# Seven block products for eight in the branch projections of a hybrid encoder trunk

## The chip, the cores and the metric

The kernel runs on one NeuronCore of a Trainium2 chip. The metric is the device time of one execution in microseconds; the times of several runs are given by their median. All arithmetic is in float32: a matrix product is done as three matmuls on rounded parts (below).

## The reference, cut to what matters

Two layers work on x (256 tokens, 2048 channels). In a layer the normalised input h is projected by w_in (2048 columns in, 14848 out) to the inputs of three token mixers and to the merge gates. Each mixer's output (256 x 1024) is multiplied by a SiLU gate, projected to 2048 channels, and the three are merged with sigmoid gates:

```
ya = einsum('bse,ed->bsd', ya * silu(rg), w_ret)     # retention, w_ret 1024 x 2048
yb = einsum('bse,ed->bsd', yb * silu(pg), w_pool)    # pooling
yc = einsum('bse,ed->bsd', yc * silu(ag), w_att)     # windowed attention
gates = sigmoid(mg).reshape(B, S, 3, D)              # mg = h @ w_in[:, 8704:]
merged = gates[:, :, 0] * ya + gates[:, :, 1] * yb + gates[:, :, 2] * yc
x = x + einsum('bsd,de->bse', merged, w_out)
```

## The kernel before, in words

**Numbers.** Every operand of a product is split into a rounded part (hi, type float32r) and the remainder (lo = value - hi); a product is a_hi w_hi + a_hi w_lo + a_lo w_hi, all added up in PSUM. For weights, ScalarE makes hi (line 208) and VectorE makes lo (line 219); activations are split by split (lines 302 to 308).

**Weight tiles.** All weights come as tiles of 128 x 1024 values (512 KB) in the order of use, which _plan writes out. SyncE loads them to four buffers (raw, line 197); there are four buffers of hi and three of lo. weights() hands out the next tile and keeps the engines ahead: when TensorE is about to use tile i, the remainder of tile i+2, the rounding of tile i+3 and the loads up to tile i+6 have been issued. A buffer is free for the next when the last reader of the one before is done, so a remainder can start when TensorE has left the tile three earlier, a rounding when it has left the tile four earlier, and a load when the remainder four earlier is made.

**Products.** gemm_n (line 310) makes 256 tokens x 512 columns: for each weight tile (two blocks of 128 rows, 512 columns) and each half t of the tokens it issues two blocks x three matmuls, 12 a tile. gemm_t makes the transposed form (channels on partitions) that some inputs want.

**Side work.** Everything else is written as generators that Side steps: each tick(), once a weight tile, lets every live task emit its next few instructions, and `yield n` makes a task wait n ticks. So small work is spread between the tiles, in the order in which it is written. Small results in PSUM (mix) use four banks in turn, and the large products two buffers of two banks (acc).

**Order of a layer.** Attention's inputs, its gate, retention's q and k, v and gate; then pooling's inputs and gates (gemm_t) with its group maps; then the merge, lines 837 to 853: for each branch (attention, retention, pooling) and each of four column blocks c of 512, the merge gate (gemm_n over eight tiles, then a sigmoid on ScalarE) and the branch projection (gemm_n over four tiles), which merge_task multiplies by the gate and adds to merged[c]. In the last branch turn_task transposes merged[c] in two halves and splits them (mt). Then the output projection (gemm_n over mt, eight tiles a column block) and the residual. The second pooling map (pool_out(1)) stands behind the first merge gate of attention.

Of the kernel before, what the change touches and what calls it, by code (L numbers as in the profile page):

```python
# [16 lines left out]
P = 128  # L17
# [15 lines left out]
N_SLOTS = 25  # L33
N_RAW, N_HI, N_LO = 4, 4, 3
N_WAKE = 9


def _plan():


    def n_tiles(name, l, c0, nk):
        return [(name, l, k2 * 256, c0, 2, 512) for k2 in range(nk // 2)]

    def t_tiles(l, c0):
        return [("w_in", l, k4 * 512, c0, 4, 256) for k4 in range(KD // 4)]

    plan = []
    for l in range(DEPTH):
        plan += n_tiles("w_in", l, OFF["akv"], KD)
        for j in range(2):  # L50
            plan += n_tiles("w_in", l, OFF["aq"] + j * 512, KD)
        for j in range(4):
            plan += t_tiles(l, OFF["ag"] + j * 256)
        for h in range(RH):
            plan += t_tiles(l, OFF["rq"] + h * RD) + t_tiles(l, OFF["rk"] + h * RD)
        for part in ("rv", "rg"):
            for j in range(2):
                plan += n_tiles("w_in", l, OFF[part] + j * 512, KD)
        for g in range(4):
            plan += t_tiles(l, OFF["pv"] + g * 256)  # L60
        for g in range(4):
            plan += t_tiles(l, OFF["pg"] + g * 256)
            if g == 2:
                plan.append(("pool_w", l, 0, 0, 4, 256))
        for b, name in ((2, "w_att"), (0, "w_ret"), (1, "w_pool")):
            for c in range(4):
                plan += n_tiles("w_in", l, OFF["mg"] + b * D + c * 512, KD)
                if b == 2 and c == 0:
                    plan.append(("pool_w", l, 512, 0, 4, 256))
                plan += n_tiles(name, l, c * 512, KW)  # L70
        for c in range(4):
            plan += n_tiles("w_out", l, c * 512, KD)
    return plan


class Side:
# [36 lines left out]
def kernel(  # L113
# [23 lines left out]
    ps_m = ctx.enter_context(tc.tile_pool(name="ps_m", bufs=4, space=PSUM))  # L137

    uid = [0]

# [19 lines left out]
    def acc(s):  # L160
        return ps_a.tile([P, 2, 512], F32, tag="acc", name=nm(s))

    def mix(s):
        return ps_m.tile([P, 512], F32, tag="mix", name=nm(s))

    side = Side()
    start, tick = side.start, side.tick
# [13 lines left out]
        return task.value  # L181


    plan = _plan()
    raws, his, los = [], [], []
    used = [0]

    def load_to(n):
        while len(raws) < min(n, len(plan)):
            i = len(raws)  # L190
            kk, w = plan[i][4:]
            raw = wp.tile([P, kk, w], F32, tag="raw", name=nm("raw"), bufs=N_RAW)
            if i == 0:
                for k in range(kk):
                    nc.sync.dma_start(out=raw[:, k], in_=weight_tiles[i][:, k * w:(k + 1) * w])
            else:
                nc.sync.dma_start(out=raw.rearrange("p k e -> p (k e)"), in_=weight_tiles[i])
            raws.append(raw)

    def hi_to(n):  # L200
        while len(his) < min(n, len(plan)):
            i = len(his)
            hi = wp.tile(list(raws[i].shape), F32R, tag="whi", name=nm("whi"), bufs=N_HI)
            if i == 0:
                for k in range(hi.shape[1]):
                    nc.vector.tensor_copy(hi[:, k], raws[i][:, k])
            else:
                nc.scalar.copy(hi, raws[i])  # L208
            his.append(hi)

    def lo_to(n):
        while len(los) < min(n, len(plan)):
# [55 lines left out]
    def ps_col(l, k):  # L268
        return cols[:, 32 + l * KW + k:32 + l * KW + k + 1]

    rope = cp.tile([P, 2, S], F32, name="rope")
# [9 lines left out]
    def rest_task():  # L281
        yield 3
        for c in range(4):
            load_x(c * 512, 512)
            yield 1
        nc.sync.dma_start(out=gains[:, 0], in_=attn_q_gain.partition_broadcast(P))
        nc.sync.dma_start(out=gains[:, 1], in_=attn_k_gain.partition_broadcast(P))
        yield 1
        nc.sync.dma_start(out=rope, in_=c_rope)
# [20 lines left out]
    def gemm_n(act, nk, early=False):  # L310

        pt = [mix("pn0"), mix("pn1")] if early else acc("pn")
        n2 = nk // 2
# [16 lines left out]
        for k2 in range(n2):  # L330
# [13 lines left out]
            if early and k2 >= n2 - 2:  # L344
                kept.append((k2, a2, hi, lo, 1))
            else:
                products(k2, a2, hi, lo, 1)
            if k2 + 1 < n2:
                tick()
        for args in kept:  # L350
# [82 lines left out]
    def scales_task(ss):  # L433
# [53 lines left out]
    for l in range(DEPTH):  # L487
# [251 lines left out]
            ut_ret += [start(retain_task(2 * j + i, rg_t)) for i in range(2)]  # L739


        def pooled_task(g, pt):
            s, _ = yield from summed(pt)
            yield 1
# [71 lines left out]
        def merge_task(b, c, pt, gs):  # L816
            yield 1
            if b == 0:
                m = slot([P, 2, 512], F32, "mrg")
                merged.append(m)  # L820
                for t in range(2):
                    nc.vector.tensor_tensor(m[:, t], pt[:, t], gs[t], ALU.mult)
                return
            m = merged[c]
            for t in range(2):
                nc.vector.tensor_tensor(gs[t], pt[:, t], gs[t], ALU.mult)
                nc.vector.tensor_tensor(m[:, t], m[:, t], gs[t], ALU.add)

        def turn_task(c, j, merge_t):
            yield from until(merge_t)  # L830
            m = merged[c]
            yield 1 + j
            pm = transposed([m[:, t, (2 * j + i) * P:(2 * j + i + 1) * P] for i in range(2) for t in range(2)], "pmt")
            yield 1
            return split_t(pm, "mt")

        merged = []
        mt_tiles = []
        for b, ut in enumerate((ut_att, ut_ret, ut_pool)):
            for c in range(4):  # L840
                pt = gemm_n(ht, KD)
                gs = []
                for t in range(2):
                    g = half([P, 512], "mg")
                    nc.scalar.activation(g, pt[:, t], AF.Sigmoid, scale=sc(t))  # L845
                    gs.append(g)
                tick()
                if b == 0 and c == 0:
                    ut_pool += pool_out(1)
                merge_t = start(merge_task(b, c, gemm_n(ut, KW), gs))  # L850
                tick()
                if b == 2:
                    mt_tiles += [start(turn_task(c, j, merge_t)) for j in range(2)]


        last = l + 1 == DEPTH
# [52 lines left out]
def _laid_out(inputs):  # L909

    import numpy as np

    a = {name: np.asarray(v) for name, v in inputs.items()}
    x = a["x"]
    plan = _plan()
    tiles = np.empty((len(plan), P, 1024), np.float32)
    for i, (name, l, r0, c0, kk, w) in enumerate(plan):
        mat = a[name][l]
        if name == "pool_w":
            mat = mat.reshape(W, 256)  # L920
        tiles[i] = mat[r0:r0 + kk * P, c0:c0 + w].reshape(kk, P, w).transpose(1, 0, 2).reshape(P, kk * w)
# [55 lines left out]
```

## Time and profile before

| | |
|---|---|
| median of 3 runs | 1813.17 us (1813.15 to 1813.53) |
| profiled execution, its own time | 1813.54 us |
| its span, first to last instruction | 1811.7 us |
| TensorE matmuls | 1803.6 us busy, 8866 instructions |
| VectorE | 1105.4 us busy |
| ScalarE | 856.5 us busy |
| GpSimd | 19.0 us busy |
| DMA | 339.53 MB, mean 187 GB/s |

Busy time is the time in which an engine has an instruction under way; TensorE's matmuls are pipelined, so one matmul's duration is longer than the distance to the next. "Idle before, releaser" in the lists is the time that an engine stood still in front of such instructions and what ended it. The trace names engines PE (TensorE), PEld (its weight loads), DVE (VectorE), ACT (ScalarE), POOL (GpSimd) and SP (SyncE).

### The profile page before, as it was taken

The numbers are of one execution on the slowest core, as the hardware profiler recorded it, in microseconds if no ns is written. First come the engines' busy times: TensorE is split into PE (matmuls) and PEld (weight loads), VectorE is DVE, ScalarE is ACT, GpSimd is POOL, SyncE is SP. The second block draws the span as 40 slices with busy tenths as digits, with TensorE's granted clock in tenths as the row PEclk, the third lists the DMA queues.
The fourth block names the chain that finished last, engine by engine and source line by source line (L and its number), as shares of the span: only waits on it lengthen the run. The fifth ranks groups of instructions, "written<-read, shape, count | busy, mean of one in ns | idle before, by whom it ended". The sixth has DMA issues, their size and how long they took to land.

```text
span 1811.7 us, 23247 instructions
## 1 busy us (share of the span) xinstructions
PE 1803.6 (100%) x8866; PEld 1522.3 (84%) x8866; DVE 1105.4 (61%) x1356; ACT 856.5 (47%) x1087; POOL 19.0 (1%) x22
## 2 busy tenths in 40 slices
PE   9999999999999999999999999999999999999999
PEld 7888888888888888888888888888888888888887
DVE  6778865676444555555567788657754454555554
ACT  6455654445444444444444555544444444444432
POOL 0000000000000000000000000000000000000000
PEclk9999999999999999999999999999999999999999
DMA  8554455455555555555555544454555556555564
GB/s 321 191 196 168 155 164 185 164 189 191 192 194 196 190 195 189 193 188 186 185 186 186 187 163 163 163 185 164 186 196 190 195 190 197 194 192 188 189 199 150
DMA packets 95951, 339.53 MB, mean 187 GB/s; under 512 B 11104, under 2 KB 11744, under 8 KB 95840
## 3 DMA queue, kind: packets, MB, share of 16 engines
q1 hardware_dynamic: 95120, 337.11, 55.8%
q8 instruction: 69, 1.13, 0.3%
q10 hardware_dynamic: 720, 0.94, 0.2%
q14 instruction: 42, 0.34, 0.1%
HBM read 335.91 MB, written 2.10 MB: 187 GB/s over the span
## 4 chain that ended last, share of the span: by engine, by line
PE 99%; DMA 1%; DVE 0%; ACT 0%; DVEq 0%; issue 0%; ACTq 0%; SPq 0%
PE pn L322 69%; PE pt L366 16%; PE pt L369 8%; DMA raw<-in_weight_tiles_dram 1%; PE ppt L394 0%; PE pmt L394 0%; PE pqt L394 0%; DMA cols<-in_columns_dram 0%; PE pro L401 0%; PE py L401 0%; PE pss L401 0%; PE py L400 0%; PE psc L400 0%; PE psc L399 0%; PE py L399 0%; PE pss L400 0%
## 5 line engine op out<-in xcount | busy, mean ns | idle before, releaser
L219 DVE TENSOR_TENSOR wlo<-raw,whi 128x1024 fp32r<-128x1024 f32 x627 | 767.4, 1224 | 626.3 <-PE pn L322 495.9
L208 ACT CAST whi<-raw 128x1024 fp32r<-128x1024 f32 x627 | 660.3, 1053 | 765.6 <-PE pn L322 569.5
L322 PE MATMUL pn<-whi,ht 128*128 128x512 f32 x2424 | 748.7, 391 | 0.1
L322 PEld LDWEIGHTS pn<-whi,ht 128*128 128x128 f32 x2424 | 454.8, 188 | 94.2 <-ACT ht L419 0.6
L322 PE MATMUL pn<-wlo,ht 128*128 128x512 f32 x1212 | 460.0, 389 | 0.4 <-DVE wlo L219 0.4
L366 PE MATMUL pt<-ht,whi 128*128 128x512 f32 x1280 | 450.4, 397 | 0.0
L369 PE MATMUL pt<-ht,wlo 128*128 128x256 f32 x1280 | 353.3, 281 | 0.0
L366 PEld LDWEIGHTS pt<-ht,whi 128*128 128x128 f32 x1280 | 238.9, 188 | 53.1
L322 PEld LDWEIGHTS pn<-wlo,ht 128*128 128x128 f32 x1212 | 227.7, 188 | 47.0 <-DVE wlo L219 0.7
L369 PEld LDWEIGHTS pt<-ht,wlo 128*128 128x128 f32 x1280 | 241.5, 189 | 2.9
L322 PE MATMUL pn<-whi,mt 128*128 128x512 f32 x512 | 158.1, 391 | 0.0
L322 PEld LDWEIGHTS pn<-whi,mt 128*128 128x128 f32 x512 | 96.1, 188 | 19.8
L322 PE MATMUL pn<-wlo,mt 128*128 128x512 f32 x256 | 97.1, 389 | 0.0
L322 PE MATMUL pn<-whi,uta 128*128 128x512 f32 x256 | 77.5, 389 | 0.0
L322 PE MATMUL pn<-whi,utp 128*128 128x512 f32 x256 | 77.5, 389 | 0.0
L322 PE MATMUL pn<-whi,utr 128*128 128x512 f32 x256 | 77.4, 389 | 0.0
L322 PEld LDWEIGHTS pn<-whi,utp 128*128 128x128 f32 x256 | 48.1, 188 | 10.0
L322 PEld LDWEIGHTS pn<-whi,utr 128*128 128x128 f32 x256 | 48.1, 188 | 9.9
L322 PEld LDWEIGHTS pn<-wlo,mt 128*128 128x128 f32 x256 | 48.1, 188 | 9.8
L322 PEld LDWEIGHTS pn<-whi,uta 128*128 128x128 f32 x256 | 47.9, 188 | 9.8
L845 ACT ACTIVATE mg<-pn,rstd 128x512 f32<-128x512 f32 x48 | 30.4, 686 | 39.7 <-PE pn L322 39.7
L384 ACT COPY tb<-pt 128x512 f32<-128x512 f32 x40 | 23.4, 585 | 54.1 <-PE pt L366 54.0
(161 smaller groups left out, 1099.1 us busy)
## 6 DMA issues: line engine op xcount, KB each, us to landing
raw<-in_weight_tiles_dram SPq DMA_DIRECT2D x627, 512.0 KB, 3.3
xa<-in_x_dram SPq DMA_DIRECT2D x4, 512.0 KB, 6.6
out_dram<-o SPq DMA_DIRECT2D x7, 256.0 KB, 4.7
xt<-in_x_t_dram SPq DMA_DIRECT2D x5, 256.0 KB, 6.7
lag<-in_c_lag_dram SPq DMA_DIRECT2D x2, 512.0 KB, 4.3
xt<-in_x_t_dram ACTq DMA_DIRECT2D x3, 256.0 KB, 6.1
raw<-in_weight_tiles_dram SPq DMA_DIRECT2D x2, 256.0 KB, 5.2
inv<-in_c_inv_dram SPq DMA_DIRECT2D x1, 512.0 KB, 4.2
```

What stands on the lines that cost most here:

```text
L208: nc.scalar.copy(hi, raws[i])
L219: nc.vector.tensor_sub(lo, raws[i], his[i].bitcast(F32))
L322: nc.tensor.matmul(pt[t] if early else pt[:, t, :], lhsT=a2[:, kk, ai, ts], rhs=w[:, kk], start=k2 == 0 and n == 0, stop=k2 == n2 - 1 and ...
L366: nc.tensor.matmul(pt[:, e, :], lhsT=hi[:, kk, es], rhs=a.rearrange("p h n -> p (h n)"), start=start, stop=stop)
L369: nc.tensor.matmul(pt[:, e, 0:S], lhsT=lo[:, kk, es], rhs=a[:, 0, :], start=False, stop=False)
L384: nc.scalar.copy(b, pt[:, :, S:2 * S])
L845: nc.scalar.activation(g, pt[:, t], AF.Sigmoid, scale=sc(t))
```

## The change

It has four parts.

**Seven products.** Columns 0 to 1023 of each branch projection (blocks c = 0 and 1) stay as they were. Columns 1024 to 2047 are taken as a 2 x 2 block product: the tokens fall into two halves, the 1024 inputs into even and odd blocks of 128, and the columns into two blocks of 512 (c = 2 and 3). product() does seven block products of 12 matmuls (P1, P2, Q5, P6, Q3, P7, Q4), each over two weight tiles with six matmuls a tile. Four of them use sums and differences of activation blocks, which combos_task makes and splits; four use sums of weight blocks. Two PSUM banks (m0, m1) hold the running sums; snap() copies a partial sum out with ScalarE, and corner_task puts a corner of the result together and merges it with its gate. During a branch only two banks are left to small work.

**Weight sums by DMA.** In the plan a use is now a tile, a sum or a chain. A "sum" is a plain load and then a DMA issued from GpSimd that adds a second tile in place. A "chain" stays in one buffer through P1, Q5, P6 and Q4: when a stage's remainder is made, an accumulating DMA from GpSimd turns it into the next stage's matrix.

**Order in a branch.** The gates of c = 2 and 3 come first, then gate and projection of c = 0 and of c = 1 (MERGE_STD), and each product stands behind the n-th standard tile of the branch (AFTER). The standard tiles of a branch are counted from 1 to 40.

**Order of the layer.** The attention branch is merged ahead of the pooling inputs, the other two behind pooling as before. The second pooling map stands behind the first gate of retention. There is one more slot of 4 KB, and the rotary table is loaded in each layer to a small buffer (half) in place of a tile of its own.

```diff
+COMBOS_AT = 8
+MERGE_STD = (("mg", 2), ("mg", 3), ("mg", 0), ("w", 0), ("mg", 1), ("w", 1))
+AFTER = {12: "P1", 14: "P2", 17: "Q5", 23: "P6", 26: "Q3", 29: "P7", 34: "Q4"}
...
     def load_to(n):
...
+            if kind == "chain":
+                _, key, stage, no, _ = uses[i]
+                if stage == 0:
+                    shape, src = tile_of(no)
+                    chains[key] = slot(shape, F32, "chain")
+                    nc.sync.dma_start(out=chains[key], in_=src)
+                raws.append(chains[key])
+                continue
...
+                nc.sync.dma_start(out=raw, in_=src)
+            if kind == "sum":
+                nc.gpsimd.dma_start(out=raw, in_=tile_of(uses[i][2])[1], accum_op=ALU.add)
...
     def lo_to(n):
...
                 nc.vector.tensor_sub(lo, raws[i], his[i].bitcast(F32))
+            if uses[i][0] == "chain" and uses[i][4] is not None:
+                nc.gpsimd.dma_start(out=raws[i], in_=tile_of(uses[i][4])[1], accum_op=ALU.add)
...
+        rope = half([P, 2, S], "rope")
+        nc.sync.dma_start(out=rope, in_=c_rope)
...
+        def corner_task(first, c, t, gates, op, a, b):
+            yield 1
+            while c not in gates:
+                yield 1
+            g = gates[c][t]
+            if op is not None:
+                part = half([P, 512], "part")
+                nc.vector.tensor_tensor(part, a, b, op)
+            else:
+                part = a
+            add_merged(first, merged[c][:, t], part, g)
+
+        def combos_task(j, ut, outs):
+            yield 1 + 2 * j
+            u = ut[j]
+            u = (yield from until(u)) if isinstance(u, Task) else u
+            s = half([P, 2, S], "us")
+            nc.vector.tensor_tensor(s, u[:, :, 0, :].bitcast(F32), u[:, :, 1, :].bitcast(F32), ALU.add)
+            c = half([P, 4, P], "uc")
+            a11, a21, a12, a22 = s[:, 0, 0:P], s[:, 0, P:S], s[:, 1, 0:P], s[:, 1, P:S]
+            nc.vector.tensor_tensor(c[:, 0], a21, a22, ALU.subtract)
+            nc.vector.tensor_tensor(c[:, 1], c[:, 0], a11, ALU.subtract)
+            nc.vector.tensor_tensor(c[:, 2], a11, a21, ALU.subtract)
+            nc.vector.tensor_tensor(c[:, 3], a12, c[:, 1], ALU.add)
+            o = slot([P, 4, 2, P], F32R, "uo")
+            split(o[:, :, 0, :], o[:, :, 1, :], c)
+            return o
...
+            def product(name):
...
+                for q in range(2):
+                    hi, lo = weights()
+                    for kk in range(2):
...
+                        for n, (ah, w) in enumerate(((a[0], hi), (a[0], lo), (a[1], hi))):
+                            nc.tensor.matmul(acc_, lhsT=ah, rhs=w[:, kk], start=fresh and q == 0 and kk == 0 and n == 0,
+                                             stop=q == 1 and kk == 1 and n == 2, skip_group_check=not fresh)
...
+            def between():
+                state["n"] += 1
+                if state["n"] == COMBOS_AT:
+                    combos.extend(start(combos_task(j, ut, combos)) for j in range(4))
+                if state["n"] in AFTER:
+                    product(AFTER[state["n"]])
...
+        merged, mt_of = {}, {}
+        merge_branch(0, ut_att)
...
+        merge_branch(1, ut_ret, late_pool)
+        merge_branch(2, ut_pool)
```

## Rows read from the trace of the kernel before

**Rows 1.** Cores' view, then the page's busy times by engine.
```profile
core 0: 1811.7 us, clock 0.999
...
PE 1803.6 (100%) x8866; PEld 1522.3 (84%) x8866; DVE 1105.4 (61%) x1356; ACT 856.5 (47%) x1087; POOL 19.0 (1%) x22
```

**Rows 2.** Waits of TensorE, whole span: us, times, longest.
```profile
PE pn L328 <- DVE whi L206: 2.6, 2, 1.4
PE pw L479 <- DVE nhalf L263: 1.1, 1, 1.1
PE pn L322 <- DVE wlo L219: 0.4, 1, 0.4
```

**Rows 3.** Chain of waits from 440 to 730 us: start, us, what.
```profile
439.88 3.63 PE pn L322 x16
443.50 0.12 PE py L399
...
446.26 0.12 PE py L401
446.38 277.47 PE pn L322 x1224
723.85 0.44 PE pmt L394 x4
724.28 2.76 PE pn L322 x12
727.05 0.44 PE pmt L394 x4
```

**Rows 4.** Windows, a stretch of the merge stage.
```profile
core 0: us, PE busy (x) PEld busy (x) DVE busy (x) ACT busy (x) POOL busy (x), PEclk, DMA share, GB/s
446.40:723.60 277.20, 277.20 (x1224) 229.50 (x1224) 143.29 (x134) 117.45 (x120) 0.00 (x0) 1.00 0.58 193
```

**Rows 5.** Groups by line and shape, VectorE and ScalarE, 446 to 724 us.
```profile
L219 DVE TENSOR_TENSOR wlo<-raw,whi 128x1024 fp32r<-128x1024 f32 x103 | 126.1, 1225 | 134.6 <-PE pn L322 128.0 <-issue 6.4
...
L784 DVE TENSOR_TENSOR utp<-y,utp 128x512 fp32r<-128x512 f32 x2 | 1.4, 684 | 0.0
L780 DVE SCALAR_TENSOR_TENSOR y<-py,cols,silu 128x256 f32<-128x256 f32 x2 | 0.9, 474 | 0.0
...
L208 ACT CAST whi<-raw 128x1024 fp32r<-128x1024 f32 x103 | 108.7, 1055 | 145.7 <-PE pn L322 133.7 <-DVE mg L826 6.0 <-DVE mrg L822 3.6
```

**Rows 6.** Waits from 446 to 724 us.
```profile
ACT whi L208 <- PE pn L322: 133.7, 76, 2.1
DVE wlo L219 <- PE pn L322: 128.0, 86, 1.8
```

**Rows 7.** Timeline of VectorE, 451 to 462 us.
```profile
454.43 1.23 DVE L219 TENSOR_TENSOR wlo<-raw,whi 128x1024 fp32r<-128x1024 f32 x1 [1.49 <-PE pn L322]
457.15 1.23 DVE L219 TENSOR_TENSOR wlo<-raw,whi 128x1024 fp32r<-128x1024 f32 x1 [1.49 <-PE pn L322]
458.30 1.28 DVE L822 TENSOR_TENSOR mrg<-pn,mg 128x512 f32<-128x512 f32 x2
```

**Rows 8.** VectorE's groups by line and shape, whole span.
```profile
L827 DVE TENSOR_TENSOR mrg<-mrg,mg 128x512 f32<-128x512 f32 x32 | 20.5, 682 | 0.0
...
L305 DVE TENSOR_TENSOR mt<-pmt,mt 128x512 fp32r<-128x512 f32 x16 | 11.1, 692 | 8.4 <-ACT mt L304 8.4
...
L729 DVE SCALAR_TENSOR_TENSOR ur<-pro,rr,rg 128x256 f32<-128x256 f32 x16 | 7.2, 479 | 4.7 <-POOL rr L410 4.7
...
L305 DVE TENSOR_TENSOR utr<-pu,utr 128x512 fp32r<-128x512 f32 x8 | 5.5, 688 | 2.5 <-ACT utr L304 2.5
...
L529 DVE TENSOR_TENSOR ra<-zn,arope 128x256 f32<-128x256 f32 x8 | 3.2, 421 | 0.1
...
L530 DVE TENSOR_TENSOR zn<-ra 128x128 f32<-128x128 f32 x4 | 1.2, 288 | 0.1
```

**Rows 9.** ScalarE's groups by line and shape, whole span.
```profile
L384 ACT COPY tb<-pt 128x512 f32<-128x512 f32 x40 | 23.4, 585 | 54.1 <-PE pt L366 54.0
...
L304 ACT CAST mt<-pmt 128x512 fp32r<-128x512 f32 x16 | 9.3, 580 | 0.0
...
L782 ACT CAST utp<-y 128x512 fp32r<-128x512 f32 x8 | 5.0, 619 | 2.4 <-DVE y L780 2.1
```

**Rows 10.** DMA issues: count, KB each, median us from issue to landing.
```profile
raw<-in_weight_tiles_dram SPq DMA_DIRECT2D x627, 512.0 KB, 3.3
xa<-in_x_dram SPq DMA_DIRECT2D x4, 512.0 KB, 6.6
```

**Rows 11.** DMA queues: packets, MB, share of 16 engines over the span.
```profile
q1 hardware_dynamic: 95120, 337.11, 55.8%
```

More of the change, by code (lines that the diff above doesn't have):

```diff
@@ L32, with tile_no @@
 PAD = 8
-N_SLOTS = 25
+N_SLOTS = 26
 N_RAW, N_HI, N_LO = 4, 4, 3
 N_WAKE = 9
+COMBOS_AT = 8
+MERGE_STD = (("mg", 2), ("mg", 3), ("mg", 0), ("w", 0), ("mg", 1), ("w", 1))
+BRANCHES = ((2, "w_att"), (0, "w_ret"), (1, "w_pool"))
+AFTER = {12: "P1", 14: "P2", 17: "Q5", 23: "P6", 26: "Q3", 29: "P7", 34: "Q4"}
 def _plan():
+    tiles, uses = [], []
+    def tile_no(name, l, rows, c0, w):
+        tiles.append((name, l, rows, c0, w))
+        return len(tiles) - 1
     def n_tiles(name, l, c0, nk):
-        return [(name, l, k2 * 256, c0, 2, 512) for k2 in range(nk // 2)]
+        return [(name, l, [k2 * 256, k2 * 256 + P], c0, 512) for k2 in range(nk // 2)]
@@ L44, in t_tiles, with use, pool_tiles, merge @@
     def t_tiles(l, c0):
-        return [("w_in", l, k4 * 512, c0, 4, 256) for k4 in range(KD // 4)]
-    plan = []
+        return [("w_in", l, [(k4 * 4 + i) * P for i in range(4)], c0, 256) for k4 in range(KD // 4)]
+    def use(ts):
+        uses.extend(("tile", tile_no(*t)) for t in ts)
+    def pool_tiles(l, g2):
+        use([("pool_w", l, [g2 * 512 + i * P for i in range(4)], 0, 256)])
+    def merge(l, b, name, late_pool):
+        quarter = {}
+        for i in range(2):
+            for j in range(2):
+                for q in range(2):
+                    quarter[i, j, q] = tile_no(name, l, [(4 * q + 2 * kk + i) * P for kk in range(2)], 1024 + 512 * j, 512)
+        n = 0
+        for what, c in MERGE_STD:
+            ts = n_tiles("w_in", l, OFF["mg"] + b * D + c * 512, KD) if what == "mg" else n_tiles(name, l, c * 512, KW)
+            for t in ts:
+                use([t])
+                n += 1
+                for q in range(2) if n in AFTER else ():
+                    stage = {"P1": 0, "Q5": 1, "P6": 2, "Q4": 3}
+                    prod = AFTER[n]
+                    if prod in stage:
+                        st = stage[prod]
+                        uses.append(("chain", (l, b, q), st, quarter[((0, 0), (0, 1), (1, 1), (1, 0))[st] + (q,)],
+                                     None if st == 3 else quarter[((0, 1), (1, 1), (1, 0))[st] + (q,)]))
+                    elif prod == "P7":
+                        uses.append(("sum", quarter[0, 1, q], quarter[1, 1, q]))
+                    else:
+                        uses.append(("tile", quarter[1, 0 if prod == "P2" else 1, q]))
+            if what == "mg" and c == 2 and late_pool:
+                pool_tiles(l, 1)
@@ L56, in _plan @@
         for part in ("rv", "rg"):
             for j in range(2):
-                plan += n_tiles("w_in", l, OFF[part] + j * 512, KD)
+                use(n_tiles("w_in", l, OFF[part] + j * 512, KD))
+        merge(l, *BRANCHES[0], False)
         for g in range(4):
-            plan += t_tiles(l, OFF["pv"] + g * 256)
+            use(t_tiles(l, OFF["pv"] + g * 256))
         for g in range(4):
-            plan += t_tiles(l, OFF["pg"] + g * 256)
+            use(t_tiles(l, OFF["pg"] + g * 256))
@@ L63, in _plan @@
             if g == 2:
[L64 to L70, printed above, removed]
+                pool_tiles(l, 0)
+        merge(l, *BRANCHES[1], True)
+        merge(l, *BRANCHES[2], False)
@@ L71, in _plan @@
         for c in range(4):
-            plan += n_tiles("w_out", l, c * 512, KD)
-    return plan
+            use(n_tiles("w_out", l, c * 512, KD))
+    return tiles, uses
 class Side:
@@ L136 @@
     ps_a = ctx.enter_context(tc.tile_pool(name="ps_a", bufs=2, space=PSUM))
-    ps_m = ctx.enter_context(tc.tile_pool(name="ps_m", bufs=4, space=PSUM))
+    ps_m = ctx.enter_context(tc.tile_pool(name="ps_m", bufs=1, space=PSUM))
     uid = [0]
@@ L161, in acc, with bank @@
         return ps_a.tile([P, 2, 512], F32, tag="acc", name=nm(s))
+    ring = ["m0", "m1", "m2", "m3"]
+    def bank(tag, s):
+        return ps_m.tile([P, 512], F32, tag=tag, name=nm(s))
     def mix(s):
-        return ps_m.tile([P, 512], F32, tag="mix", name=nm(s))
+        ring.append(ring.pop(0))
+        return bank(ring[-1], s)
     side = Side()
@@ L181, in until, with tile_of @@
         return task.value
-    plan = _plan()
+    tiles, uses = _plan()
     raws, his, los = [], [], []
     used = [0]
+    chains = {}
+    def tile_of(n):
+        _, _, rows, _, w = tiles[n]
+        return [P, len(rows), w], weight_tiles[n].rearrange("p (k e) -> p k e", k=len(rows))
     def load_to(n):
-        while len(raws) < min(n, len(plan)):
+        while len(raws) < min(n, len(uses)):
             i = len(raws)
-            kk, w = plan[i][4:]
-            raw = wp.tile([P, kk, w], F32, tag="raw", name=nm("raw"), bufs=N_RAW)
+            kind = uses[i][0]
+            if kind == "chain":
[6 more added lines that the diff above has]
+                continue
+            shape, src = tile_of(uses[i][1])
+            raw = wp.tile(shape, F32, tag="raw", name=nm("raw"), bufs=N_RAW)
             if i == 0:
-                for k in range(kk):
-                    nc.sync.dma_start(out=raw[:, k], in_=weight_tiles[i][:, k * w:(k + 1) * w])
-            else:
-                nc.sync.dma_start(out=raw.rearrange("p k e -> p (k e)"), in_=weight_tiles[i])
+                for k in range(shape[1]):
+                    nc.sync.dma_start(out=raw[:, k], in_=src[:, k])
+            else:
+                nc.sync.dma_start(out=raw, in_=src)
+            if kind == "sum":
+                nc.gpsimd.dma_start(out=raw, in_=tile_of(uses[i][2])[1], accum_op=ALU.add)
             raws.append(raw)
     def hi_to(n):
-        while len(his) < min(n, len(plan)):
+        while len(his) < min(n, len(uses)):
             i = len(his)
@@ L211, in lo_to @@
     def lo_to(n):
-        while len(los) < min(n, len(plan)):
+        while len(los) < min(n, len(uses)):
             i = len(los)
@@ L308, in split, with gemm_n @@
             nc.vector.scalar_tensor_tensor(dst_lo, src, scale, dst_hi.bitcast(F32), ALU.mult, ALU.subtract)
-    def gemm_n(act, nk, early=False):
+    def gemm_n(act, nk, early=False, between=None):
         pt = [mix("pn0"), mix("pn1")] if early else acc("pn")
@@ L347, in gemm_n @@
                 products(k2, a2, hi, lo, 1)
+            if between:
+                between()
             if k2 + 1 < n2:
@@ L739, with add_merged, merge_task @@
             ut_ret += [start(retain_task(2 * j + i, rg_t)) for i in range(2)]
+        def add_merged(first, m, part, gate):
+            if first:
+                nc.vector.tensor_tensor(m, part, gate, ALU.mult)
+            else:
+                nc.vector.tensor_tensor(gate, part, gate, ALU.mult)
+                nc.vector.tensor_tensor(m, m, gate, ALU.add)
+        def merge_task(first, c, pt, gs):
+            yield 1
+            for t in range(2):
+                add_merged(first, merged[c][:, t], pt[:, t], gs[t])
@@ new lines, in corner_task @@
+        def corner_task(first, c, t, gates, op, a, b):
+            yield 1
+            while c not in gates:
+                yield 1
+            g = gates[c][t]
+            if op is not None:
+                part = half([P, 512], "part")
+                nc.vector.tensor_tensor(part, a, b, op)
+            else:
+                part = a
[15 more added lines that the diff above has]
+            return o
@@ new lines, in turn_task, with merge_branch, snap, corner @@
+        def turn_task(c, j, done):
+            for task in done:
+                yield from until(task)
+            m = merged[c]
+            yield 1 + j
+            pm = transposed([m[:, t, (2 * j + i) * P:(2 * j + i + 1) * P] for i in range(2) for t in range(2)], "pmt")
+            yield 1
+            return split_t(pm, "mt")
+        def merge_branch(which, ut, late_pool=None):
+            first, last = which == 0, which == 2
+            gates, combos, snaps, done = {}, [], {}, {}
+            state = {"n": 0}
+            ring[:] = ["m2", "m3"]
+            def snap(name, src):
+                snaps[name] = held([P, 512], name)
+                nc.scalar.copy(snaps[name], src)
+            def corner(c, t, op, a, b):
+                if c not in merged:
+                    merged[c] = slot([P, 2, 512], F32, "mrg")
+                done[c, t] = start(corner_task(first, c, t, gates, op, a, b))
+            def product(name):
+                if name == "P1":
+                    state["x"] = bank("m0", "px")
+                if name in ("P2", "Q5"):
+                    state["v"] = bank("m1", "pv")
+                acc_ = state["x"] if name in ("P1", "P6", "P7", "Q4") else state["v"]
+                fresh = name in ("P1", "P2", "Q5")
+                for q in range(2):
+                    hi, lo = weights()
+                    for kk in range(2):
+                        j = 2 * q + kk
+                        if name in ("P1", "P2", "Q4"):
+                            i, t = {"P1": (0, 0), "P2": (1, 0), "Q4": (1, 1)}[name]
+                            u = need(ut[j])
+                            a = [u[:, i, h, t * P:(t + 1) * P] for h in range(2)]
+                        else:
+                            u = need(combos[j])
+                            a = [u[:, ("Q5", "P6", "P7", "Q3").index(name), h] for h in range(2)]
+                        for n, (ah, w) in enumerate(((a[0], hi), (a[0], lo), (a[1], hi))):
+                            nc.tensor.matmul(acc_, lhsT=ah, rhs=w[:, kk], start=fresh and q == 0 and kk == 0 and n == 0,
+                                             stop=q == 1 and kk == 1 and n == 2, skip_group_check=not fresh)
+                if name == "P1":
+                    snap("p1", acc_)
+                elif name == "P2":
+                    corner(2, 0, ALU.add, acc_, snaps["p1"])
+                elif name == "Q5":
+                    snap("q5", acc_)
+                elif name == "P6":
+                    snap("u2", acc_)
+                elif name == "Q3":
+                    corner(3, 0, ALU.subtract, acc_, snaps["u2"])
+                elif name == "P7":
+                    snap("u3", acc_)
+                    corner(3, 1, ALU.subtract, snaps["q5"], snaps["u3"])
+                else:
+                    corner(2, 1, None, acc_, None)
+            def between():
[4 more added lines that the diff above has]
+                    product(AFTER[state["n"]])
+            for what, c in MERGE_STD:
+                if what == "mg":
+                    pt = gemm_n(ht, KD, between=between)
+                    gates[c] = []
+                    for t in range(2):
+                        g = held([P, 512], "mg") if c >= 2 else half([P, 512], "mg")
+                        nc.scalar.activation(g, pt[:, t], AF.Sigmoid, scale=sc(t))
+                        gates[c].append(g)
+                    tick()
+                    if c == 2 and late_pool:
+                        late_pool()
+                else:
+                    if c not in merged:
+                        merged[c] = slot([P, 2, 512], F32, "mrg")
+                    pt = gemm_n(ut, KW, between=between)
+                    done[c, 0] = done[c, 1] = start(merge_task(first, c, pt, gates[c]))
+                    tick()
+                    if last:
+                        for j in range(2):
+                            mt_of[c, j] = start(turn_task(c, j, [done[c, 0]]))
+            if last:
+                for c in (2, 3):
+                    for j in range(2):
+                        mt_of[c, j] = start(turn_task(c, j, [done[c, 0], done[c, 1]]))
+            ring[:] = ["m0", "m1", "m2", "m3"] if not last else ring
+            return
@@ L813, with late_pool @@
                 ut_pool += pool_out(0)
[L816 to L853, printed above, removed]
+        def late_pool():
+            ut_pool.extend(pool_out(1))
+        merge_branch(1, ut_ret, late_pool)
+        merge_branch(2, ut_pool)
+        ring[:] = ["m0", "m1", "m2", "m3"]
+        mt_tiles = [mt_of[c, j] for c in range(4) for j in range(2)]
         last = l + 1 == DEPTH
@@ L914, in _laid_out @@
     x = a["x"]
-    plan = _plan()
+    plan, _ = _plan()
     tiles = np.empty((len(plan), P, 1024), np.float32)
-    for i, (name, l, r0, c0, kk, w) in enumerate(plan):
+    for i, (name, l, rows, c0, w) in enumerate(plan):
         mat = a[name][l]
@@ L920, in _laid_out @@
             mat = mat.reshape(W, 256)
-        tiles[i] = mat[r0:r0 + kk * P, c0:c0 + w].reshape(kk, P, w).transpose(1, 0, 2).reshape(P, kk * w)
+        for k, r0 in enumerate(rows):
+            tiles[i][:, k * w:(k + 1) * w] = mat[r0:r0 + P, c0:c0 + w]
     rows = np.concatenate([a["norm_g"].reshape(DEPTH * KD, P), a["pool_scale"].reshape(DEPTH * KW, P)])
```

11 lines of the change are left out of this document (4 added, 7 removed).

## The prediction

> **What bounds the kernel now.** I read the cores' view and the page's busy table first: TensorE is busy in 1803.6 of 1811.7 us at a granted clock of 0.999 [rows 1], the upper of its two levels. A busy share alone doesn't say that TensorE sets the pace, so the next views are the waits and the chain of waits. In the whole span TensorE waits 4.1 us for others, all at the start [rows 2], and in the chain 1224 matmuls of the merge stage follow each other in one piece of 277.47 us [rows 3]. That piece gives the price of a 512-column matmul: 277.47 / 1224 = 226.7 ns. (The 389 ns of the lists is one pipelined matmul from start to end, and would make the saving 1.7 times too large.) A weight tile of 12 such matmuls lasts 2.72 us, one of 6 lasts 1.36 us.
>
> Then the stretch's other engines: VectorE is busy for 143.29 and ScalarE for 117.45 of 277.20 us [rows 4], with one remainder (wlo) of 1.22 us and one rounding (whi) of 1.06 us per tile [rows 5]. Both mostly wait for TensorE to give a buffer back [rows 6]: the timeline shows a remainder starting just when TensorE changes tiles, with 1.49 us idle before it [rows 7]. So wherever TensorE loses matmuls and nobody else comes late, the end moves by 226.7 ns for each.
>
> **The change part by part.**
>
> *Products.* For columns 1024 to 2047 a branch now runs seven block products of 12 matmuls where it ran eight: 12 fewer in each of six branches (three branches, two layers), 72 in all. 72 x 226.7 ns = 16.3 us less. The stationary and moving shapes and the bank changes stay as they were, so I take the same price for a product's matmul.
>
> *Tiles.* Each product uses a tile for six matmuls only, so a branch splits 14 tiles there where it split 8: six more remainders and roundings, 36 in all, 44 us of VectorE and 38 of ScalarE. A short tile leaves VectorE 1.36 - 1.22 = 0.14 us and ScalarE 0.30, where a standard tile leaves 1.50 and 1.66. No stretch of short tiles is longer than two, and remainders are made two tiles ahead, so alone they cost nothing.
>
> *Combinations.* Once in each branch, for each of four activation tiles, combos_task adds the halves (0.69 us, as the 128x512 rows), does four 128x128 operations (0.28 each), waits for a ScalarE rounding (0.62 and a hand-over of 0.1) and subtracts (0.69) [rows 8, 9]: 3.2 us of VectorE's queue, all between the 9th and the 16th standard tile of the branch. The first corner adds 0.69 and two merge operations, back to back 1.28 us for two [rows 7], 1.9 in all. That is 4 x 3.2 + 1.9 = 14.7 us, against free time of nine standard and four short tiles up to Q5: 9 x 1.50 + 4 x 0.14 = 14.1. The 0.6 that is lacking is less than the lead, which is smallest in front of two short tiles: 2.72 - 1.22 = 1.5 us. So nothing in the attention and pooling branches. In the retention branch late_pool falls into the same tiles: four operations of 0.47 us (y), two of 0.68 (utp) and the pool tile's remainder of 1.22 [rows 5, 8] are 4.5 us, against 24 matmuls from 443.50 to 446.38, 2.9 us [rows 3]. It lacks 0.6 + 1.6 = 2.2 us with a lead of 1.5: 0.7 us in each layer, 1.4 in all. The bounds are 0, if the rounding's wait is filled with a remainder, and some 5 us over six branches, if the small operations take the 0.42 of a 128x256 row [rows 8] (2.2 us more a branch, of which about 1.4 is covered).
>
> *Snaps and later corners.* Four PSUM copies a branch of 0.59 us on ScalarE [rows 9], and two more corners between standard tiles, lie beside TensorE's work. They cost nothing as long as VectorE's 52% of this stretch doesn't pass some 70: per branch 54 x 1.22 + 13 + 19 x 0.69 = 92 us of 564 x 226.7 ns = 128 us.
>
> *Accumulating DMAs.* The trace has none: GpSimd issues no DMA at all. In the chain, a remainder must end before the next matrix is added in place, and the next stage's rounding waits for that. From P1's second remainder to Q5's second rounding TensorE works through four short and three standard tiles, 13.6 us, less half a microsecond; from Q5 to P6 two short and four standard, the same. So the chain has about 13 us.
>
> The sums of P7 are tighter. Their plain load waits for a raw buffer: the second one's is free when the remainder of standard tile 27 ends, which starts when TensorE leaves tile 26. From there to P7's second tile lie Q3 (2.72), tiles 27 to 29 (8.16) and P7's first (1.36): 12.24 us. Of these go the remainder 1.22, the load 3.3 [rows 10], rounding and remainder 2.28 and three hand-overs of 0.1: 5.1 us are left for the accumulation from issue to landing. The first has 13.6 - 7.1 = 6.5.
>
> How long does it take? From below 3.3, the plain load of the same tile; from above 6.6, the load of as many bytes in the crowd at the start [rows 10], and 1.57 for a second stream of 512 KB, 8.2. (1.57 us is a plain tile's share of the 16 engines: 55.8% of 1811.7 us for 337.11 MB, or 643 tiles [rows 11].) The nearest row is the plain load, so I build on it: 3.3, 1.57 because the tile is read as well as written, and half of one other load that lands meanwhile, 0.8: 5.7 us. It is 0.6 us late in a branch, 3.6 us over six. At 3.3 it costs nothing; at 8.2 3.1 us a branch, 18.6. While ScalarE waits for the sum at the head of its queue, the roundings of tiles 30 and on stand behind it, and VectorE's remainders and the merge of column block 0 behind those; TensorE has three tiles in hand. On GpSimd's queue only accumulations stand behind an accumulation: the square roots of the retention heads come earlier in their branch.
>
> The Trainium skill (DMA: Bandwidth & Descriptors, section Anatomy of one DMA, SWDGE path) fits a DMA issued from GpSimd with 2.0 us and its bytes over 436 GB/s: an estimate of 3.2 us for 512 KB, without an accumulation. By that figure the sums would never be late and the total below would be 3.6 us better; no run so far shows such a DMA.
>
> *Order of the output projection.* Column block 1 is now merged last, and the projection reads it at its third tile. Its transposes, and those of blocks 2 and 3, are emitted together after the second tile: six groups of 0.44 us [rows 3] with four banks, so the fifth waits for the first split. From the end of tile two: transpose 0.44, rounding 0.58, remainder 0.69 and hand-overs bring the first split to 2.0 us, the second to 2.6; with the fifth and sixth transposes behind them TensorE goes on at 3.1, or at 3.5 when ScalarE is amid a weight tile, which I take. The transposes themselves, 2.6, were paid before too: 0.9 us a layer, 1.8 in all (bounds 0 and 4).
>
> *At nothing:* attention's merge ahead of pooling (the tail of retention heads 2 and 3 moves from the pooling projections beside the gates, where VectorE idles half the time; uncovered, half of the eight utr and 16 ur operations is 6.3 us [rows 8]); the rotary table loaded once a layer (256 KB on SyncE's queue, which runs four tiles ahead); two PSUM banks for small work in a branch (heads start two tiles apart).
>
> **Sum.** Against the profiled execution's 1813.54 us: -16.3 + 1.4 + 3.6 + 1.8 = -9.5, so 1804.0. The median of the runs is 0.4 lower: 1803.7.
>
> **The rivals.**
>
> *The sum at P7 is late: slower.* Place: ScalarE's rounding of P7's two tiles. With the rest as above the gain is used up at (16.3 - 3.2) / 6 = 2.2 us a branch, an accumulation of 7.3 us; at 8.2 the time is 1813.2 - 16.3 + 3.2 + 18.6 = 1818.7. For it: two sums and three plain loads want the DMA engines within some 8 us, and at 3.1 us a sum this is 2 x 3.1 + 3 x 1.57 = 10.9 us of work. Against it: SyncE's next load waits for these very buffers, which thins the crowd. The Trainium skill (the same page, section Issuing engines are not separate DMA queues) says that DMAs of all issuers share the 16 engines and interleave; by that rule the 8.2 is nearer than the 3.3, and this rival gets its weight from the crowd just counted.
>
> *The DMA engines become the bound.* 48 plain tiles of 1.57 are 75 us of a branch's 128; eight accumulations fill the rest at 6.6 us of engine time each. At 8 they make a branch 11 us longer, 1866 or so. Against it: the share is 0.58 [rows 4], and 6.6 is four times a plain tile.
>
> *VectorE is late around P1 to Q5.* With 5 us there on top, and 4 at the projection, 1811: nearly no change. For it: 14.7 against 14.1 us is a close fit. Against it: a wait of TensorE also lets VectorE catch up.
>
> *The matmuls are saved and nothing waits.* 1813.2 - 16.3 = 1796.9.
>
> **How the numbers follow.** A measurement of this kernel can tell about 0.2%, 3.6 us, from no change. Forecast as worked out, with accumulations between 4.5 and 6.6 us, its own range 1797 to 1809: 0.50. Nothing waits: 0.08. Sum late: 0.25, of it 0.20 slower and 0.05 within. VectorE late: 0.13, of it 0.04 faster, 0.08 within and 0.01 slower. DMA engines: 0.04, slower. Faster 0.62, within 0.13, slower 0.25. The range takes in all waits at nothing (1796) and accumulations of 8.2 us with VectorE's 5 on top (1824); outside are the DMA rival and a sum beyond 8.2.
>
> **What would show it.** 8794 matmuls, VectorE near 1220 and ScalarE near 925 us busy; in the merge stage pieces of the chain broken only at P7 (by whi from a DMA), at the retention branch's first products (by wlo) and at the third tile of the output projection. The accumulations' time to landing decides: under 5.1 us the first rival is dead, above 7.3 the forecast is. I am wrong too if a product's matmul costs other than 226.7 ns, or if TensorE waits in the chain's stages (Q5, P6, Q4), which 13 us should cover.

## The result and the profile after

The change made the kernel slower: 1832.26 us (median of 4 runs, 1830.8 to 1837.69) against 1813.35, a ratio of 1.011 with a 95% interval of 1.0088 to 1.0131. Forecast was 1803.7, range 1796 to 1824. The profiled execution took 1830.8 us with a span of 1829.0.

The page's busy times answer to [rows 1]:

```profile
PE 1800.4 (98%) x8794; PEld 1512.3 (83%) x8794; DVE 1206.9 (66%) x1554; ACT 917.6 (50%) x1171; POOL 60.2 (3%) x70
```

The 72 matmuls are gone (8794) and VectorE and ScalarE have the work that was forecast (1220 and 925). But TensorE now stands still for 1829.0 - 1800.4 = 28.6 us where it was 8.1. Its waits over the whole span, as in [rows 2], say where:

```profile
PE px L893 <- ACT whi L271: 13.9, 9, 3.5
PE px L893 <- DVE wlo L282: 6.3, 9, 0.8
PE pn L390 <- DVE whi L269: 1.5, 2, 0.9
PE pn L384 <- DVE wlo L282: 1.1, 2, 0.8
```

Line 893 is the matmul of product(), px the bank of P1, P6, P7 and Q4. The chain of waits of the pooling branch of the first layer, 760 to 800 us (compare [rows 3]), shows which of them:

```profile
761.21 2.72 PE px L893 x12
763.93 5.45 PE pn L384 x24
...
769.47 1.24 DVE wlo L282
770.70 0.02 issue
770.72 4.26 DMA raw<-in_weight_tiles_dram
...
775.62 9.67 DMA raw<-in_weight_tiles_dram
785.29 0.02 issue
...
785.39 1.05 ACT whi L271
786.45 0.02 issue
786.47 1.24 DVE wlo L282
787.70 0.04 issue
787.75 5.06 PE px L893 x11
792.81 3.07 PE pn L384 x12
```

It has the links that the prediction set up for the sum of P7: a remainder frees the raw buffer, the plain load follows (4.26 us), then the accumulation (9.67 us), a rounding, a remainder, and only then P7. This chain runs through the first of P7's two sums. In the two attention branches the chain runs through the second, on which the prediction built; in the first layer:

```profile
402.35 7.95 PE pn L384 x35
...
411.63 3.18 DMA raw<-in_weight_tiles_dram
...
415.43 8.80 DMA raw<-in_weight_tiles_dram
...
425.41 1.24 DVE wlo L282
...
426.69 1.42 PE px L893 x5
```

In the pooling branch, from the end of P6 (763.93) to the end of P7 (792.81) it takes 28.88 us. Without a wait it is three standard tiles, Q3, three standard tiles and P7, 8 x 2.72 = 21.76 us; 7.12 us are lost.

The same two points in the six branches, by the chain's pieces or the timeline (us): 402.35 to 428.11, 630.13 to 657.85, 763.93 to 792.81, 1312.65 to 1338.99, 1541.03 to 1566.69, 1673.16 to 1701.18. Less 21.76 each they lose 4.0, 6.0, 7.1, 4.6, 3.9 and 6.3, together 31.8 us. The span is 17.3 us longer though 16.3 us of matmuls went, 33.6 in all: nearly all of it is at P7.

Part of it is the clock. Windows around this P7 (columns as in [rows 4]):

```profile
778.00:783.00 5.00, 4.97 (x22) 3.77 (x21) 0.00 (x0) 0.00 (x0) 0.88 (x1) 1.00 0.87 214
783.00:788.00 5.00, 1.02 (x2) 0.51 (x3) 1.53 (x2) 1.34 (x2) 0.00 (x0) 0.86 0.57 115
788.00:793.00 5.00, 5.00 (x12) 3.84 (x13) 5.00 (x7) 3.86 (x5) 0.00 (x0) 0.50 0.60 210
793.00:798.00 5.00, 5.00 (x25) 4.11 (x24) 4.89 (x7) 2.97 (x4) 0.00 (x0) 0.96 0.87 309
```

After TensorE waited 3.5 us in one piece its granted clock is 0.50, the lower level, from 788 to 793 us, and 12 matmuls run where 22 do at the upper level (778 to 783 us). P7's last 11 matmuls take 5.06 us there; at 226.7 ns they would take 2.5.

The DMA issues, as in [rows 10], and the queue of GpSimd, as in [rows 11]:

```profile
q0 software_dynamic: 6912, 25.17, 7.7%
```

```profile
raw<-in_weight_tiles_dram SPq DMA_DIRECT2D x615, 512.0 KB, 3.4
chain<-in_weight_tiles_dram POOLq DMA_DIRECT2D x36, 512.0 KB, 5.4
...
raw<-in_weight_tiles_dram POOLq DMA_DIRECT2D x12, 512.0 KB, 8.9
```

The chain's 36 accumulations land in 5.4 us, close to the 5.7 on which the sum was made. P7's 12, of the same form and size, take 8.9.

### The profile page after: what moved, and what is told of

It reads as the page before. It is cut to its first block, busy times and chain, and to the rows that moved or that the text cites. A ratio compares the mean times of both kernels' runs of the same rounds, so it can differ in the third digit from the quotient of the medians.

```text
span 1829.0 us, 23536 instructions
## 1 busy us (share of the span) xinstructions
PE 1800.4 (98%) x8794; PEld 1512.3 (83%) x8794; DVE 1206.9 (66%) x1554; ACT 917.6 (50%) x1171; POOL 60.2 (3%) x70
## 4 chain that ended last, share of the span: by engine, by line
PE 92%; DMA 5%; issue 1%; DVE 1%; ACT 0%; ACTq 0%; SPq 0%; DVEq 0%; POOLq 0%
PE pn L384 58%; PE pt L430 16%; PE pt L433 8%; DMA raw<-in_weight_tiles_dram 4%; PE px L893 4%; PE pv L893 2%; DVE wlo L282 1%; ACT whi L271 0%; DMA xt<-in_x_t_dram 0%; PE pmt L458 0%; PE ppt L458 0%; PE pqt L458 0%; PE py L465 0%; PE pro L465 0%; PE pss L465 0%
## 5 line engine op out<-in xcount | busy, mean ns | idle before, releaser
L282 DVE TENSOR_TENSOR wlo<-raw,whi 128x1024 fp32r<-128x1024 f32 x615 | 750.8, 1223 | 492.3 <-PE pn L384 302.6
L271 ACT CAST whi<-raw 128x1024 fp32r<-128x1024 f32 x615 | 645.6, 1052 | 649.4 <-PE pn L384 364.7
L282 DVE TENSOR_TENSOR wlo<-chain,whi 128x1024 fp32r<-128x1024 f32 x48 | 58.7, 1224 | 47.4 <-PE pn L384 39.9
L271 ACT CAST whi<-chain 128x1024 fp32r<-128x1024 f32 x48 | 50.7, 1056 | 52.8 <-PE pn L384 50.3
L284 POOL DMA_DIRECT2D chain<-in_weight_tiles_dram x36 | 31.6, 877 | 736.3 <-DVE wlo L282 697.6
L893 PE MATMUL px<-whi,uo 128*128 128x512 f32 x96 | 37.7, 452 | 13.9 <-ACT whi L271 13.9
L384 PE MATMUL pn<-whi,utr 128*128 128x512 f32 x128 | 39.1, 389 | 0.0
L384 PE MATMUL pn<-whi,uta 128*128 128x512 f32 x128 | 39.1, 389 | 0.0
```

The source lines that it names most:

```text
L284: nc.gpsimd.dma_start(out=raws[i], in_=tile_of(uses[i][4])[1], accum_op=ALU.add)
L384: nc.tensor.matmul(pt[t] if early else pt[:, t, :], lhsT=a2[:, kk, ai, ts], rhs=w[:, kk], start=k2 == 0 and n == 0, stop=k2 == n2 - 1 and ...
L893: nc.tensor.matmul(acc_, lhsT=ah, rhs=w[:, kk], start=fresh and q == 0 and kk == 0 and n == 0, stop=q == 1 and kk == 1 and n == 2, skip_gr ...
```

## The experiments

Theory A is that the whole loss is at P7. Rival B is that it is spread (DMA traffic of the chain, a full VectorE) and merely comes out there. Each run was compared with the kernel before on the same chip (median 1813.5 us in the first four runs, 1813.3 in the others).

**E1: P7 without its sums.** Each of its tiles is one block alone, so the product leaves out the other block.

```diff
-uses.append(("sum", quarter[0, 1, q], quarter[1, 1, q]))
+uses.append(("tile", quarter[1, 1, q]))
```

> P7's two tiles are plain loads of one weight block in place of the sum of two (the product is then taken with that block alone); all else is as in the changed kernel. Theory A, the whole loss arises at P7, where the sum comes late: TensorE's waits at P7 and the slow clock behind them go, and the time is 1797 to 1800 us (1813.2 less 16.3, and a little). Rival B, the loss is spread (DMA engines shared with the 36 accumulations of the chain, VectorE too full around P1 to Q5) and P7 is only where it comes out: the waits move to other products, time 1812 or more.

Measured: 1798.08 us (1797.89 to 1799.36), ratio 0.9918 (0.9903 to 0.9933). TensorE's waits in the whole span:

```profile
PE pn L390 <- DVE whi L269: 1.9, 2, 1.2
PE pw L545 <- DVE nhalf L328: 1.1, 1, 1.1
PE pn L384 <- DVE wlo L282: 0.4, 1, 0.4
PE pn L384 <- ACT ht L483: 0.2, 1, 0.2
```

Nothing waits any more around the products or at the output projection, with the chain's 36 accumulations, all combinations and the new order in place. Rival B falls. The chain of the first branch now runs through P7:

```profile
402.13 8.16 PE pn L384 x36
410.29 2.72 PE pv L893 x12
413.01 8.16 PE pn L384 x36
421.17 2.72 PE px L893 x12
423.89 13.60 PE pn L384 x60
```

From 402.13 to 423.89 it is 21.76 us, the price worked out above.

**E2: the sums by VectorE.** Both blocks are loaded plainly to two raw buffers and added ahead of the rounding; load_to counts buffers, so that no more than four are in use.

```diff
-nc.gpsimd.dma_start(out=raw, in_=tile_of(uses[i][2])[1], accum_op=ALU.add)
+seconds[i] = wp.tile(shape, F32, tag="raw", name=nm("raw"), bufs=N_RAW)
+nc.sync.dma_start(out=seconds[i], in_=tile_of(uses[i][2])[1])
...
+if i in seconds:
+    nc.vector.tensor_tensor(raws[i], raws[i], seconds.pop(i), ALU.add)
 nc.scalar.copy(hi, raws[i])
```

> P7's sums are made by VectorE from two plain loads (12 more operations of 1.22 us, 15 us of VectorE; both blocks take a raw buffer), not by an accumulating DMA. Theory A: the second load is there 4.7 us after TensorE leaves tile 26, the sum, rounding and remainder are made by 11.1 of the 12.2 us, no wait: 1797 to 1803 us. Rival B: VectorE gets fuller and the DMA load stays, 1815 or more.

Measured: 1801.91 us, ratio 0.9938 (0.9926 to 0.9951). As theory A has it, but for 2.6 us of waits at P7:

```profile
PE px L903 <- DVE wlo L292: 2.6, 5, 0.8
```

**E3: one accumulation at P7.** Why 8.9 us? The first thought (A1) was the two accumulations side by side, with plain loads. The run leaves the second block out of P7's second tile.

```diff
+uses.append(("sum", ...) if q == 0 else ("tile", quarter[1, 1, q]))
```

> Only the first of P7's two tiles is a sum by an accumulating DMA, the second is a plain load of one block (the product is then taken with that block for half of its depth). Theory A1, the accumulation takes 8.9 us because two of them and three plain loads crowd the DMA engines: its time to landing falls to 5.5 to 7 us, less than the 6.5 that the first tile has less 1.0 for a slower plain load, or just over it, time 1797 to 1806. Theory A2, an accumulation onto a freshly loaded buffer takes 8.9 us by itself: it stays at 8 to 9, late by 3 us in each of six branches, 1815 or more.

Measured: 1829.26 us, ratio 1.009 (1.0076 to 1.0103), and the one that is left is no faster. Its instructions and their time to landing, by its line:

```profile
L260 POOL DMA_DIRECT2D raw<-in_weight_tiles_dram x6: 862/868/872, 413.7 to 1686.7; - x6
...
DMA to landing us min/median/max: 8.7/9.1/9.3
```

So a second accumulation isn't needed, and A1 falls. A2 (slow by itself onto a freshly loaded buffer) stood, and a third was formed: A3, the plain loads beside it. At P7 loads were issued at 411.6, 413.0 and 414.3 us, around the accumulations at 413.2 and 415.4; in the changed kernel, by line and window:

```profile
L258 SPq DMA_DIRECT2D raw<-in_weight_tiles_dram x1: 328/328/328, 414.3 to 414.3; - x1
...
DMA to landing us min/median/max: 9.0/9.0/9.0
```

```profile
L284 POOL DMA_DIRECT2D chain<-in_weight_tiles_dram x1: 875/875/875, 376.5 to 376.5; - x1
...
DMA to landing us min/median/max: 5.5/5.5/5.5
```

The first is a plain load at P7, itself 9.0 us instead of 3.4. The second is an accumulation of the chain at 376.5 us: no load is issued between 373.5 and 381.9 there.

But "beside" needs care. The chain's next accumulation has three loads beside it and isn't slow; the loads are:

```profile
L284 POOL DMA_DIRECT2D chain<-in_weight_tiles_dram x1: 875/875/875, 379.6 to 379.6; - x1
...
DMA to landing us min/median/max: 5.4/5.4/5.4
```

```profile
L258 SPq DMA_DIRECT2D raw<-in_weight_tiles_dram x3: 328/328/328, 381.9 to 384.4; - x3
...
DMA to landing us min/median/max: 4.6/5.8/5.8
```

These loads are issued 2.3 to 4.8 us behind it. In the whole span no plain load is issued within 2 us of any of the chain's 36 accumulations, while at P7 one is issued within 0.3 us of the first sum in each branch, and is still under way when the second starts. So it seems to matter when a load is issued, and not only how many run beside the accumulation. No run varies that distance alone: this is a reading of the traces and not shown.

**E4: the chain without its accumulations.** Its four stages all use the first block, so the sums of the chain are left out.

```diff
-if uses[i][0] == "chain" and uses[i][4] is not None:
-    nc.gpsimd.dma_start(out=raws[i], in_=tile_of(uses[i][4])[1], accum_op=ALU.add)
```

> The 36 accumulations of the chain are left out (its four stages all use the first block); P7's 12 sums stay. Theory A: the waits at P7 stay as they are, 1828 to 1835 us. Rival B, the chain's traffic delays the others: 1815 or less.

Measured: 1831.53 us, ratio 1.0103 (1.009 to 1.0117), P7's sums at 8.7 us. The chain neither costs time nor slows P7.

**E5: the loads behind the sums are held.** Ahead of each of these loads SyncE's queue gets a small copy that reads a sum and so waits until it has landed.

```diff
+for k in (1, 2, 3):
+    if kind == "tile" and i >= 3 and uses[i - k][0] == "sum":
+        nc.sync.dma_start(out=raw[:, 0, 2 * k:2 * k + 2], in_=raws[i - k][:, 0, 0:2])
 nc.sync.dma_start(out=raw, in_=src)
```

> As the changed kernel, but the three plain loads behind P7's two sums are held on SyncE's queue until both accumulations have landed (each waits for small copies that read the sums). Theory A3, an accumulation is slow where plain loads of SyncE's queue are under way beside it (three are, at P7; none for the first microseconds in the chain, where it lands in 5.4): the 12 accumulations land in 5.4 to 7 us. Rival A2, an accumulation onto a freshly loaded buffer is slow by itself: they stay at 8 to 9. The time is of little use (the held loads come late in their turn), 1815 to 1850.

Measured in a single run: 1849.05 us. The sums' landing:

```profile
L263 POOL DMA_DIRECT2D raw<-in_weight_tiles_dram x12: 865/870/875, 413.5 to 1703.7; - x12
DMA to landing us min/median/max: 5.4/6.0/7.4
```

Same accumulation, same buffer, two at a time: 6.0 us instead of 8.9 once the loads behind them are held. A3 stands, A2 falls. The time is worse because the held loads come late: TensorE's waits for the roundings of standard tiles grow from 0.3 us to 15.9.

**E6: P7 later.**

```diff
-AFTER = {12: "P1", 14: "P2", 17: "Q5", 23: "P6", 26: "Q3", 29: "P7", 34: "Q4"}
+AFTER = {12: "P1", 14: "P2", 17: "Q5", 23: "P6", 26: "Q3", 32: "P7", 35: "Q4"}
```

> P7 stands behind standard tile 32 in place of 29 and Q4 behind 35 in place of 34, so five standard tiles lie between Q3 and P7 instead of three, and the loads come every 2.7 us there, not every 1.4. Theory A3: 2.7 us more for the sums and fewer loads beside them, an accumulation of 6.5 to 7.5 us against some 7 to 8 left, late by 0 to 0.5 us a branch, 1797 to 1806 us. Rival A2, 8.9 us whatever lies beside it: late by 1 to 2 us in each branch and a slow clock behind the longer ones, 1807 to 1815.

Measured: 1828.21 us, ratio 1.0081 (1.0064 to 1.0098). Neither theory's time was met. The sums land in 5.5 to 10.5 us, median 8.8, although the loads come half as often. That is A2's number and not the 6.5 to 7.5 of A3, but E5 speaks against A2. The chain of the first branch shows the same two links:

```profile
414.48 4.63 DMA raw<-in_weight_tiles_dram
...
419.66 9.39 DMA raw<-in_weight_tiles_dram
```

Loads 2.7 us apart are still three or so beside an accumulation that takes 9 us. The one sum that landed in 5.5 us, at 781.7 us, had no load issued from 1.4 us ahead of it to 2.2 us behind it. A sum by DMA needs a place where no load is issued close to it, as far as these traces tell, or more lead than these buffers give.

**E7: sums by VectorE and P7 later** (the edits of E2 and E6).

> The sums by VectorE and the later place of P7 together. If what is left of the sum by VectorE is its fit at P7 (2.6 us of waits for remainders and the unevenness behind them), 1797 to 1800 us; if it is VectorE's 15 us of extra work as such, 1800 to 1803 as with the sums by VectorE alone.

Measured: 1799.13 us (1797.9 to 1799.52), ratio 0.9921 (0.9906 to 0.9936): faster than both kernels. TensorE's wait for remainders at the products is down to 0.6 us, so what E2 lacked was mostly its fit at P7 and not VectorE's work.

**E8: the order alone.** The kernel before with attention merged ahead of pooling, and pool_out(1) behind retention's first gate.

> The kernel before with one part of the change alone: attention is merged ahead of pooling's inputs, and the second pooling map stands behind retention's first gate. All theories here: no change, 1812 to 1815 us. If the order of the layer has a price or a gain of its own, it shows.

Measured: 1813.66 us against 1813.29, ratio 1.0002 (0.9993 to 1.0012). No price and no gain.

## Why the prediction was wrong

**The products: right.** Forecast 16.3 us less; with P7's sum out of the way (E1) it is 1813.47 - 1798.08 = 15.4, all other costs included.

**The combinations (1.4) and the projection's order (1.8): too high, both about 0.** E1 shows no wait at either. VectorE waited for the combinations' rounding in only 4 of 24 cases; in the others a remainder filled the gap, which was the lower bound given. The pieces that would have been worth 3.2 us of loss are 0.9 in E1, all told.

**The chain: right.** 13 us of room were forecast against accumulations of 5.4 us, at most 7.1; E4 shows that it costs nothing.

**The sum of P7: this step failed, by its size.** The place, the order of the links and the room (5.1 us) were right, and the rival built on it is what happened. The term was "3.3, 1.57 because the tile is read as well as written, and half of one other load that lands meanwhile, 0.8: 5.7 us". The first two add up to 4.9, near the 5.4 of the chain's accumulations; the engine time was right too, 7.7% of 1829.0 us over 48 is 2.9 us for a forecast of 3.1. What failed was the half load. Two or three whole loads lie beside it, and the accumulation then lands in 8.9 us; the load ahead of it also lands later in four of the six branches (4.3 in the pooling chain above, 3.3 forecast), and 0.6 us pass between its landing and the accumulation's start, where the prediction had 0.1 for a hand-over. The rival counted the crowd, 10.9 us of engine work within some 8 us, and the sum should have been made with that. Its upper bound of 8.2 us came from the crowd at the start of the kernel, without an accumulation in it, and with it the range ended too low.

Over the six branches the second sum's load averages 4.06 us, the step to its accumulation 0.60 and the accumulation 8.76. In the prediction's own sum that is 0.76 + 0.50 + 3.66 = 4.92 us late a branch, 29.5 over six; the chains lost 31.8.

**A term that was missing: the clock.** In three of the six branches TensorE waited some 3 us in one piece (3.1, 3.5 and 2.7 us for the rounding) and then ran P7 at the lower level for a while: 11 matmuls in 4.32, 5.06 and 5.06 us for 2.5. That is 6.9 us more, but not all of it is lost to the clock, since at the upper level TensorE would have waited for the second sum. In the other three branches P7 ends 1.5 us after the second block's remainder, in these three 2.0, 2.8 and 2.6 us after it (timeline). So an estimate of the clock's price within P7 is 3 us, and with the 29.5 it makes up what was lost. No part of the prediction priced what a stop of TensorE costs beyond its length.

One long wait isn't even needed. In E6 the granted clock fell in four of the six branches, with no wait at P7 longer than 1.8 us. In the first layer's retention branch it fell behind waits of 0.9 and 0.8 us with a single matmul between them (columns as in [rows 4]):

```profile
655.00:659.50 4.50, 3.09 (x13) 2.00 (x11) 1.05 (x1) 1.04 (x1) 0.00 (x0) 1.00 0.75 204
660.00:663.00 3.00, 2.90 (x6) 1.41 (x5) 0.80 (x1) 1.87 (x2) 0.00 (x0) 0.50 0.51 180
```

The Trainium skill (DMA: Bandwidth & Descriptors, section Anatomy of one DMA, SWDGE path) gives an estimate of 3.2 us for a DMA of this size issued from GpSimd; with an accumulation the trace doesn't agree, 5.4 us in the chain and 8.9 at P7. What the same page of the Trainium skill says in the section Issuing engines are not separate DMA queues, that all issuers share the engines and interleave, agrees with the trace at P7: the plain load beside the sums took 9.0 us instead of 3.4.

## What to carry to other kernels

Taking matmuls from a kernel that TensorE bounds pays by the distance between matmuls, if every operand still comes in time; so count for each new kind of load the room from the moment its buffer is free to the moment TensorE wants it, and price the load with all the transfers that run beside it at that place, those issued at about the same moment above all, and not with its median elsewhere. A load that is a chain of two DMAs has the latency of both, and needs its buffer that much earlier or another engine to add. And a wait of TensorE of about 3 us, or here two of 0.9 and 0.8 us close together, can cost more than its length, since the matmuls behind it may run at the lower clock.

## What the runs showed of the hardware that was not expected

An accumulating DMA of 512 KB to SBUF lands in 5.4 us (median, 5.1 to 7.1) when no plain load is issued within 2 us of it, even with three loads issued behind that, which land in 5.0 us (median) instead of 3.4. It lands in 8.9 us (median) at P7, where a load is issued within 0.3 us of the first sum and is still under way when the second starts (6.0 when the loads behind were held). A second accumulation beside it made no difference that was seen (9.1 us without it at P7). It takes 2.9 us of the 16 engines against 1.57 for a plain load of the same size. GpSimd itself is busy for 0.87 us with each.
